# Hidden first pair reloaded for its sums, first product split by chunks, raw weight chunks loaded into the sums' tiles, side copies pinned

## The chip, the cores and the metric

The kernel runs on one NeuronCore of one Trainium2 chip. The metric is the device time of one launch in microseconds. TensorE (PE in the profile) multiplies, VectorE (DVE), ScalarE (ACT) and GpSimd (POOL) work beside it, and SyncE (SP) issues nearly all DMA transfers, in the order of its queue.

## The reference, cut to what matters

One layer of a decoder trunk on 1024 prompt tokens and 64 sample tokens, width 1024: a half-step SwiGLU feed-forward, a token mixer of two branches, a second half-step feed-forward, and a final norm. All in fp32.

```python
def swiglu(x, w_in, w_out):               # D_MODEL 1024, D_FF 2816
    gu = x @ w_in
    g, u = gu[..., :D_FF], gu[..., D_FF:]
    return (jax.nn.silu(g) * u) @ w_out
...
        x = x + 0.5 * swiglu(rmsnorm(x, norm_ffn1[l]), ffn1_w_in[l], ffn1_w_out[l])
...
            rmsnorm(x, norm_mix[l]), pool_hist, out_pos0, conv_hist, h0, w_in[l], pool_w_group[l],
...
    y_prompt = rmsnorm(xp, norm_final)
    y_sample = rmsnorm(xs, norm_final)
```

## The kernel before, in words

**Numbers.** Every fp32 operand is split into a rounded part (`hi`, `hh`, `wh`: ACT copies it to the type fp32r) and a rest (`lo`, `hr`, `wl`: DVE subtracts). A product is three matmuls: high by high, low by high, high by low. Weights arrive by DMA as "raw" chunks (`wraw`, a ring of N_RAW = 6), become `wh` on ACT and `wl` on DVE (rings of N_W = 3 each), and are used once.

**Stages.** By the trace: operands and some plain products of the first feed-forward up to about 105 us; the rest of its first matrix product (`ffn_in`) to 544; `second`, its second matrix product, to 788; the mixer to 2174; the second feed-forward's `ffn_in` to about 2655, its `second` to about 2885; the final norm to the end. Both feed-forwards run the same code. The tokens are worked in two halves h of 512 and 576, each again cut in two so that seven products of a Strassen-Winograd scheme take the place of eight.

**The hidden rows.** For each block ff of 128 hidden columns `hidden` gets the tile g (`L691`). Even blocks go to DRAM at once (a "put" into `hblock`), odd blocks too, and `hidden_odd` then starts a chain `sums` (`L707`): four subtractions in place on the even and odd tiles, each issued H_PACE after the last, then two more puts. A chain is a generator with a due time on a clock that counts PE's issued matmul columns (`pe[0]`); `tick` runs the chain that is due first. The four subtractions run on POOL, except for the first pair (ff == 1), where they run on DVE (`L713`). The last pair is held back (`hlast`) and worked at the start of `second`.

**The second product.** `second` runs the products in the order 1, 2, 5, 6, 4, 7, 3. Each has four units m, each unit 11 steps of k in three chunks of 4, 4 and 3. In a step six matmuls are issued, three for each half. By the trace a unit takes 8.25 us, a chunk of four steps 3.0 us. `fetch_X` (`L731`) issues the loads of a product's operands from `hblock`, tiles `hr` and `hp`, and `split_X` (`L747`) splits them: `hh` on ACT (`L750`), the rest in place on DVE (`L751`). `weights` (`L773`) makes the weights: product 5 adds two raw chunks on POOL (`L785`) into a tile ws that is held, product 6 subtracts another raw chunk from it in place (`L789`), `fourth` (`L800`) turns the held tile into the weights of product 3 in place, and product 7 subtracts two raw chunks into a tile of a ring `wsum` of N_S = 4 (`L794`). `old` (`L812`) adds an earlier part of the result, reloaded as `xo`. `parts` (`L767`, `L768`) then makes `wh` and `wl`.

**Side work.** `part` (`L307`) loads chunks of the mixer's weights during `ffn_in`, waits PART_W, splits them (`ph` by ACT through `split`, `L357`; the rest by DVE, `L359`) and puts both parts in DRAM for the mixer.

**The order.** A scheduler orders each engine's instructions by dependences and priorities; `tc.keep_in_program_order` holds an instruction at its place in the program, `tc.high_priority` moves one ahead. On a queue an instruction that waits holds up all behind it: SP's loads too. `norm_parts` makes the mixer's operands of one half (`L1022`), beginning with the PE sums `pss` of the squares `ssq` (`L386`).

## Time and profile before

| | |
|---|---|
| three runs | 2931.96, 2939.40, 2940.15 us; median 2939.40, mean 2937.17 |
| the profiled execution | 2934.26 us, its span 2932.5 us |
| PE busy | 2793.1 us, 95% of the span |
| DVE, ACT, POOL busy | 1876.5, 1399.6, 1349.2 us |
| mean granted PE clock | 0.982 |
| DMA | 512.47 MB, 175 GB/s over the span |

The span is the profiled execution from its first to its last instruction; what lies around it is 1.8 us. In rows of the timeline a start and a duration come first, then engine, source line, operation and tiles; in brackets stands the idle time of that engine ahead of the row, and what ended it. In rows of windows stand the window, its length, the busy time of PE, of PE's weight loads, DVE, ACT and POOL (with counts), the granted clock, the mean busy share of the DMA engines, and GB/s.

### The profile page before, as it was taken

The page shows a single profiled execution, that of the slowest core. Times are in us where ns is not written, and L with a number is a line of the kernel's source. Part 1 is how long each engine was busy: PE and PEld are TensorE (multiplying, and loading weights), DVE is VectorE, ACT ScalarE, POOL GpSimd, SP SyncE. Part 2 cuts the span into 40 slices and gives each one's busy share as a digit, 9 for nine tenths or more (in the row PEclk, how much of TensorE's full clock was granted, in tenths as well). Part 3 has the DMA queues.
Part 4 walks back from the last instruction along what each step waited for, and adds up shares of the span by engine and source line. Part 5 has one row for each costly group of instructions (what it writes and reads, how often), then busy time and mean ns, then how long its engine had stood idle before and what let it go on. Part 6 is the DMA issues. An engine that isn't in the chain of part 4 may idle for free. (4 is left out here: it accounts for less than half of the span.)

```text
span 2932.5 us, 54478 instructions
## 1 busy us (share of the span) xinstructions
PE 2793.1 (95%) x19834; PEld 2614.3 (89%) x19834; DVE 1876.5 (64%) x2864; ACT 1399.6 (48%) x3086; POOL 1349.2 (46%) x1408
## 2 busy tenths in 40 slices
PE   7999999899999999999989999898999999999998
PEld 6988899899889999999988887677998999998987
DVE  6665554676884486866766767866665554555865
ACT  5444444443454555554546567566233444444434
POOL 5455566345542364554622332323234665561651
PEclk9999999999999999999999999999999999999999
DMA  4576542687545455543366667786774332335873
GB/s 124 163 237 199 183 133 93 185 239 224 184 114 166 158 173 179 183 136 127 103 239 195 191 227 234 252 256 188 232 240 144 101 108 89 100 122 179 243 240 109
DMA packets 564749, 512.47 MB, mean 175 GB/s; under 512 B 37748, under 2 KB 433384, under 8 KB 564472
## 3 DMA queue, kind: packets, MB, share of 16 engines
q1 hardware_dynamic: 564464, 508.98, 55.4%
q8 instruction: 156, 2.56, 0.4%
q14 instruction: 113, 0.93, 0.1%
q10 hardware_dynamic: 16, 0.00, 0.0%
HBM read 361.28 MB, written 147.80 MB: 174 GB/s over the span
## 5 line engine op out<-in xcount | busy, mean ns | idle before, releaser
L166 PE MATMUL pw<-X,wh 128*128 128x288 f32 (+2 forms) x2832 | 625.9, 310 | 3.8 <-ACT v L566 3.5
L166 PEld LDWEIGHTS pw<-X,wh 128*128 128x128 f32 x2832 | 461.5, 189 | 25.6 <-ACT v L566 4.2
L166 PE MATMUL pw<-X,wl 128*128 128x288 f32 (+1 forms) x1644 | 473.2, 288 | 0.9 <-DVE wl L450 0.9
L166 PE MATMUL pw<-hl,wh 128*128 128x256 f32 (+1 forms) x1536 | 393.9, 329 | 6.2 <-DVE t L570 6.2
L450 DVE TENSOR_TENSOR wl<-s,wh 128x512 fp32r<-128x512 f32 x288 | 234.0, 813 | 257.1 <-ACT wh L449 233.3
L443 POOL TENSOR_TENSOR s<-wraw,wraw 128x512 f32<-128x512 f32 x144 | 194.2, 1349 | 336.0 <-DVE wl L450 204.8
L166 PE MATMUL pw<-hi,wl 128*128 128x288 f32 x1120 | 330.8, 295 | 5.1 <-DVE wl L450 5.1
L166 PE MATMUL pw<-hi,wh 128*128 128x288 f32 x1120 | 332.1, 297 | 2.8 <-DVE t L604 2.8
L166 PE MATMUL pw<-lo,wh 128*128 128x288 f32 x1120 | 330.5, 295 | 0.0
L166 PEld LDWEIGHTS pw<-X,wl 128*128 128x128 f32 x1644 | 311.2, 189 | 1.1 <-DVE wl L450 1.1
L166 PE MATMUL pw<-hl,wl 128*128 128x256 f32 x1072 | 301.2, 281 | 0.0
L166 PEld LDWEIGHTS pw<-hl,wh 128*128 128x128 f32 x1536 | 259.8, 190 | 28.1 <-DVE t L570 7.3
L450 DVE TENSOR_TENSOR wl<-wraw,wh 128x512 fp32r<-128x512 f32 x216 | 189.4, 877 | 139.7 <-ACT wh L449 131.5
L449 ACT ACTIVATE wh<-s 128x512 fp32r<-128x512 f32 x288 | 181.1, 630 | 163.6 <-PE pw L166 138.9
L166 PEld LDWEIGHTS pw<-hi,wh 128*128 128x128 f32 x1120 | 211.5, 189 | 9.8 <-DVE t L604 3.5
L166 PEld LDWEIGHTS pw<-hi,wl 128*128 128x128 f32 x1120 | 211.0, 188 | 5.3 <-DVE wl L450 5.3
L166 PEld LDWEIGHTS pw<-lo,wh 128*128 128x128 f32 x1120 | 211.6, 189 | 0.0
L449 ACT ACTIVATE wh<-wraw 128x512 fp32r<-128x512 f32 x216 | 135.5, 628 | 157.6 <-PE pw L166 140.2
L166 PEld LDWEIGHTS pw<-hl,wl 128*128 128x128 f32 x1072 | 203.9, 190 | 0.0
L166 PE MATMUL po<-hh,wl 128*128 128x256 f32 (+1 forms) x848 | 186.8, 292 | 8.6 <-DVE wl L768 8.6
L166 PE MATMUL po<-hh,wh 128*128 128x256 f32 (+1 forms) x848 | 187.1, 291 | 3.8 <-ACT wh L767 3.8
L166 PE MATMUL po<-hr,wh 128*128 128x256 f32 (+1 forms) x848 | 186.2, 290 | 0.0
(399 smaller groups left out, 6839.0 us busy)
## 6 DMA issues: line engine op xcount, KB each, us to landing
wraw<-in_ffn_w_in_dram SPq DMA_DIRECT2D x188, 256.0 KB
wraw<-in_ffn_w_out_dram SPq DMA_DIRECT2D x144, 256.0 KB
wraw<-in_w_in_dram SPq DMA_DIRECT2D x144, 256.0 KB
wh<-part SPq DMA_DIRECT2D x116, 256.0 KB
wl<-part SPq DMA_DIRECT2D x116, 256.0 KB
hr<-hb SPq DMA_DIRECT2D x106, 272.0 KB
hb<-g SPq DMA_DIRECT2D x66, 288.0 KB
hb<-g SPq DMA_DIRECT2D x66, 256.0 KB
```

Of the source, the lines that this page charges most:

```text
L166: T.matmul(out, lhsT, rhs, start=start, stop=stop, skip_group_check=free)
L443: G.tensor_tensor(t, a, b, op=op)
L449: S.activation(wh, a, AF.Copy)
L450: V.tensor_tensor(wl, a, wh.bitcast(F32), op=ALU.subtract)
```

## The change

Six edits, all in both feed-forwards:

1. Of the first pair of hidden blocks both halves of g are put in DRAM at once ("18" and "23" instead of "1" and "23"). A chain `again` starts 100 units of the PE clock later for half 0 and 115 later for half 1: it loads both tiles again (two DMAs for each half), waits H_LOAD = 5, and then runs the sums on POOL, as for all other pairs. DVE has no hidden sums left.
2. H_AT, the delay of the sums' chains, goes from 3 to 4.
3. In `part` the ACT copy is an `AF.Copy` with its place pinned; before it was an `AF.Identity` that the scheduler placed. Counted in the built order, the ACT copy of the chunk for which ACT waits at 345.56 us stood 18 matmuls behind its load's issue before, and stands 61 behind it now. Most others move from 17 to 25 matmuls to 36 to 65; a few stay at 17.
4. In product 1, unit 0, the operands are split by chunks: k 0 to 3 ahead of the unit, k 4 to 7 ahead of its second chunk, the rest ahead of its third.
5. Product 5 loads its first raw chunk into the tile ws and adds the second one in place. Product 7 and `fourth` load one of theirs into a `wsum` tile. So a sum takes one slot of the raw ring and not two, and `fourth` none.
6. `norm_parts` of half 1 for the mixer starts 3.0 later.

```diff
@@ -43,7 +43,7 @@
-H_AT, H_PACE, H_OUT = 3.0, 0.5, 3.0
+H_AT, H_PACE, H_OUT, H_AGAIN, H_LOAD = 4.0, 0.5, 3.0, 100.0, 5.0
 AHEAD = {'2': 11, '5': 11, '6': 8, '4': 8, '7': 10, '3': 10}
...
 STEP_S = 1.0
@@ -303,6 +303,7 @@
         return wh.rearrange("p (k c) -> p k c", c=ncol), wl.rearrange("p (k c) -> p k c", c=ncol)
...
     parted, nth = {}, [0]
+    pin = tc.keep_in_program_order
...
@@ -312,7 +313,8 @@
                 w[k0 * P : (k0 + nk) * P, c0 : c0 + P].rearrange("(k p) c -> p k c", p=P))
...
             a = fx(F32R, "ph")[:, : nk * P]
-            split(t, a, t.bitcast(F32R))
+            pin(S.activation(a, t, AF.Copy))
+            V.tensor_tensor(t.bitcast(F32R), t, a.bitcast(F32), op=ALU.subtract)
             to = [dp.tile([P, nk * P], F32, tag=nm("part"), name=nm("part")) for _ in range(2)]
...
             dma(to[1], t)
@@ -677,8 +679,8 @@
-    for ps_ in ("1", "23", "75", "46"):
-        for i in range(NK2):
+    for i in range(NK2):
+        for ps_ in ("1" if i else "18", "23", "75", "46"):
             t = dp.tile([P, len(ps_), N2], F32, tag=f"hb{ps_}_{i}", name=f"hb{ps_}_{i}")
...
             for j, p in enumerate(ps_):
@@ -687,36 +689,48 @@
+        n, at = NPAIR[h], HALF_AT[h]
         if ff == NFF - 1:
             hlast.append(lambda: hidden_odd(h, ff, g))
+        elif ff == 1:
+            put(h, 0, "23", g)
+            hsums.append(start(again(h), H_AGAIN + 15.0 * h))
         elif ff % 2:
             hidden_odd(h, ff, g)
+        elif ff:
+            even[h] = g
+            dma(hblock["1", ff // 2][:, at : at + n], g[:, :n])
         else:
-            even[h] = g
-            n, at = NPAIR[h], HALF_AT[h]
-            dma(hblock["1", ff // 2][:, at : at + n], g[:, :n])
+            put(h, 0, "18", g)
+
+    def put(h, i, ps_, x):
+        n, at = NPAIR[h], HALF_AT[h]
+        return dma(hblock[ps_, i][:, :, at : at + n], x[:, : 2 * n].rearrange("p (a t) -> p a t", a=2))
+
+    def again(h):
+        n, at = NPAIR[h], HALF_AT[h]
+        e, g = fx(name="e"), fx(name="g")
+        for t, ps_ in ((e, "18"), (g, "23")):
+            dma(t[:, : 2 * n].rearrange("p (a t) -> p a t", a=2), hblock[ps_, 0][:, :, at : at + n])
+        yield H_LOAD
+        yield from pair_sums(h, 0, e, g)
...
-        n, i, at = NPAIR[h], ff // 2, HALF_AT[h]
+        put(h, ff // 2, "23", g)
+        hsums.append(start(pair_sums(h, ff // 2, even[h], g), H_AT))
+
+    def pair_sums(h, i, e, g):
+
+        n = NPAIR[h]
         f, s_ = slice(0, n), slice(n, 2 * n)
-
-        def put(ps_, x):
-            return dma(hblock[ps_, i][:, :, at : at + n], x[:, : 2 * n].rearrange("p (a t) -> p a t", a=2))
-
-        e = even[h]
-        put("23", g)
-
-        def sums():
-            for out, a, b in ((e[:, s_], e[:, s_], e[:, f]), (g[:, s_], g[:, s_], e[:, s_]),
-                              (e[:, f], g[:, s_], e[:, f]), (g[:, f], g[:, f], g[:, s_])):
-                tc.keep_in_program_order((V if ff == 1 else G).tensor_tensor(out, a, b, op=ALU.subtract))
-                yield H_PACE
-            yield H_OUT
-            for ps_, x in (("75", e), ("46", g)):
-                tc.keep_in_program_order(put(ps_, x))
-
-        hsums.append(start(sums(), H_AT))
+        for out, a, b in ((e[:, s_], e[:, s_], e[:, f]), (g[:, s_], g[:, s_], e[:, s_]),
+                          (e[:, f], g[:, s_], e[:, f]), (g[:, f], g[:, f], g[:, s_])):
+            pin(G.tensor_tensor(out, a, b, op=ALU.subtract))
+            yield H_PACE
+        yield H_OUT
+        for ps_, x in (("75", e), ("46", g)):
+            pin(put(h, i, ps_, x))
...
@@ -747,11 +761,12 @@
         def split_X(below=NK2):
...
                 _, r, a = raws.pop(0)
-                tc.keep_in_program_order(S.activation(a, r, AF.Copy))
+                pin(S.activation(a, r, AF.Copy))
                 V.tensor_tensor(r.bitcast(F32R), r, a.bitcast(F32), op=ALU.subtract)
-        def raw(par, mh, m, kb, nk):
-            t = sp.tile([P, 4 * P], F32, tag="wraw", bufs=N_RAW, name=nm("wraw"))[:, : nk * P]
+        def raw(par, mh, m, kb, nk, t=None):
+            if t is None:
+                t = sp.tile([P, 4 * P], F32, tag="wraw", bufs=N_RAW, name=nm("wraw"))[:, : nk * P]
             c0 = (mh * 4 + m) * P
...
             return t
@@ -780,7 +795,7 @@
                     a = raw(*{"1": (0, 0), "2": (1, 0), "4": (1, 1)}[p], m, kb, nk)
...
                     a = held[m, kb] = act((P, 4 * P), name="ws")[:, : nk * P]
-                    x, y = raw(0, 1, m, kb, nk), raw(1, 1, m, kb, nk)
+                    x, y = raw(0, 1, m, kb, nk, a), raw(1, 1, m, kb, nk)
                     with tc.high_priority(hp[0]):
...
                 elif p == "6":
@@ -789,14 +804,15 @@
                         G.tensor_tensor(a, a, x, op=ALU.subtract)
...
                     a = stage["p"].tile([P, 4 * P], F32, tag="wsum", bufs=N_S, name=nm("ws"))[:, : nk * P]
-                    x, y = raw(0, 0, m, kb, nk), raw(0, 1, m, kb, nk)
+                    x, y = raw(0, 0, m, kb, nk, a), raw(0, 1, m, kb, nk)
                     with tc.high_priority(hp[0]):
...
             for kb, nk in chunks:
-                a, x = held[m, kb], raw(1, 0, m, kb, nk)
+                t = stage["p"].tile([P, 4 * P], F32, tag="wsum", bufs=N_S, name=nm("ws"))[:, : nk * P]
+                a, x = held[m, kb], raw(1, 0, m, kb, nk, t)
                 G.tensor_tensor(a, x, a, op=ALU.subtract)
...
         def old(m, q, col):
@@ -816,7 +832,9 @@
         def unit(p, m, hs, ws):
...
             for kb, nk, wh, wl in ws:
-                if kb == 8 and len(hs) == 2:
+                if kb and len(hs) == 2 and (p, m) == ("1", 0):
+                    split_X(kb + 4)
+                elif kb == 8 and len(hs) == 2:
                     split_X()
...
                     k = kb + kk
@@ -864,13 +882,14 @@
                 add(a[:, s_], a[:, s_])
...
         fetch_X("1", NK2)
-        split_X()
+        split_X(4)
         while hlast:
...
         for p, nxt in zip(order[:-1], order[1:]):
-            split_X(8)
+            if p != "1":
+                split_X(8)
             fetch_X(p, NK2)
...
                 if p == "6":
@@ -1025,7 +1044,7 @@
         o = []
...
         finish(c)
-        prep1m[h] = start(norm_parts(xt, h, i_gm, o, (0.5, 1.2)[h], s), 0.0), o
+        prep1m[h] = start(norm_parts(xt, h, i_gm, o, (0.5, 1.2)[h], s), (0.0, 3.0)[h]), o
...
```

How the built order moves, at three places. New line numbers are higher: `L783` is the old `L768`, `L765` the old `L751`, `L771` the old `L756`, `L757` the old `L743`, `L800` the old `L785`, `L804` the old `L789`. Behind an arrow stand the operands.

VectorE at the start of product 1 in the first feed-forward, before: `hr` are the operands' rests, `wl` of 128x512 and 128x384 the weights of the second and third chunk of unit 0.

```order
L751 TENSOR_TENSOR hr_6300<-hr_6300,hh_6299 128x544
L751 TENSOR_TENSOR hr_6303<-hr_6303,hh_6302 128x544
L609 TENSOR_TENSOR g_6176<-g_6176,pw_1090_6162 128x288
L751 TENSOR_TENSOR hr_6306<-hr_6306,hh_6305 128x544
L751 TENSOR_TENSOR hr_6309<-hr_6309,hh_6308 128x544
L751 TENSOR_TENSOR hr_6312<-hr_6312,hh_6311 128x544
L751 TENSOR_TENSOR hr_6315<-hr_6315,hh_6314 128x544
L751 TENSOR_TENSOR hr_6318<-hr_6318,hh_6317 128x544
L751 TENSOR_TENSOR hr_6321<-hr_6321,hh_6320 128x544
L751 TENSOR_TENSOR hr_6324<-hr_6324,hh_6323 128x544
L768 TENSOR_TENSOR wl_6397<-wraw_6394,wh_6396 128x512
L768 TENSOR_TENSOR wl_6427<-wraw_6424,wh_6426 128x384
```

The same place in the changed kernel:

```order
L783 TENSOR_TENSOR wl_6361<-wraw_6358,wh_6360 128x512
L608 TENSOR_TENSOR g_6184<-pw_1106_6230,t_6183 128x288
L765 TENSOR_TENSOR hr_6308<-hr_6308,hh_6307 128x544
L765 TENSOR_TENSOR hr_6311<-hr_6311,hh_6310 128x544
L611 TENSOR_TENSOR g_6184<-g_6184,pw_1094_6170 128x288
L783 TENSOR_TENSOR wl_6391<-wraw_6388,wh_6390 128x512
L783 TENSOR_TENSOR wl_6429<-wraw_6426,wh_6428 128x384
L765 TENSOR_TENSOR hr_6314<-hr_6314,hh_6313 128x544
L765 TENSOR_TENSOR hr_6317<-hr_6317,hh_6316 128x544
L765 TENSOR_TENSOR hr_6320<-hr_6320,hh_6319 128x544
L765 TENSOR_TENSOR hr_6323<-hr_6323,hh_6322 128x544
L783 TENSOR_TENSOR wl_6470<-wraw_6467,wh_6469 128x512
```

The `wl` of chunks 2 and 3 stood behind all eleven `hr`; now they stand behind the fourth, and the `hr` of k 4 to 7 behind them.

SyncE's queue ahead of product 7 in the first feed-forward, before: 8518 to 8524 are the raw chunks of the last `fourth`, 8542 and 8544 the two of product 7's first sum, 8576 to 8612 those of its second and third.

```order
L756 DMA wraw_8518<-in_ffn_w_out_dram 128x4x128
L756 DMA wraw_8521<-in_ffn_w_out_dram 128x4x128
L756 DMA wraw_8524<-in_ffn_w_out_dram 128x3x128
L756 DMA wraw_8542<-in_ffn_w_out_dram 128x4x128
L743 DMA hr_8414<-hb_6_294 128x544
L743 DMA hr_8417<-hb_7_295 128x544
L743 DMA hr_8420<-hb_8_296 128x544
L756 DMA wraw_8544<-in_ffn_w_out_dram 128x4x128
L756 DMA wraw_8576<-in_ffn_w_out_dram 128x4x128
L756 DMA wraw_8578<-in_ffn_w_out_dram 128x4x128
L756 DMA wraw_8610<-in_ffn_w_out_dram 128x3x128
L756 DMA wraw_8612<-in_ffn_w_out_dram 128x3x128
```

The same stretch in the changed kernel: 8420 to 8480 are the last weights of product 4, 8539 to 8605 the second raw chunks of product 7's first three sums, 8658 to 8724 those of its unit 1.

```order
L771 DMA wraw_8420<-in_ffn_w_out_dram 128x4x128
L771 DMA wraw_8450<-in_ffn_w_out_dram 128x4x128
L771 DMA wraw_8480<-in_ffn_w_out_dram 128x3x128
L771 DMA wraw_8539<-in_ffn_w_out_dram 128x4x128
L771 DMA wraw_8572<-in_ffn_w_out_dram 128x4x128
L771 DMA wraw_8605<-in_ffn_w_out_dram 128x3x128
L771 DMA wraw_8658<-in_ffn_w_out_dram 128x4x128
L757 DMA hr_8410<-hb_6_292 128x544
L757 DMA hr_8413<-hb_7_296 128x544
L757 DMA hr_8416<-hb_8_300 128x544
L771 DMA wraw_8691<-in_ffn_w_out_dram 128x4x128
L771 DMA wraw_8724<-in_ffn_w_out_dram 128x3x128
```

The first raw chunks of unit 0's three sums (into `wsum` tiles) and the last `fourth`'s three stand 20 and more rows further ahead now; three loads of `hr` stand behind the four second chunks instead of ahead of them.

POOL in products 5 and 6 of the first feed-forward, before: 7520 to 7588 are the sums of product 5's unit 3, `L789` the subtractions of product 6.

```order
L785 TENSOR_TENSOR ws_7440<-wraw_7441,wraw_7443 128x512
L785 TENSOR_TENSOR ws_7474<-wraw_7475,wraw_7477 128x384
L785 TENSOR_TENSOR ws_7520<-wraw_7521,wraw_7523 128x512
L785 TENSOR_TENSOR ws_7554<-wraw_7555,wraw_7557 128x512
L785 TENSOR_TENSOR ws_7588<-wraw_7589,wraw_7591 128x384
L789 TENSOR_TENSOR ws_7178<-ws_7178,wraw_7638 128x512
L789 TENSOR_TENSOR ws_7212<-ws_7212,wraw_7669 128x512
L789 TENSOR_TENSOR ws_7246<-ws_7246,wraw_7700 128x384
L789 TENSOR_TENSOR ws_7290<-ws_7290,wraw_7750 128x512
```

And in the changed kernel, where 7519 to 7585 are the same three sums of unit 3:

```order
L804 TENSOR_TENSOR ws_7328<-ws_7328,wraw_7777 128x512
L804 TENSOR_TENSOR ws_7361<-ws_7361,wraw_7808 128x384
L804 TENSOR_TENSOR ws_7408<-ws_7408,wraw_7860 128x512
L804 TENSOR_TENSOR ws_7441<-ws_7441,wraw_7891 128x512
L800 TENSOR_TENSOR ws_7519<-ws_7519,wraw_7521 128x512
L800 TENSOR_TENSOR ws_7552<-ws_7552,wraw_7554 128x512
L800 TENSOR_TENSOR ws_7585<-ws_7585,wraw_7587 128x384
L804 TENSOR_TENSOR ws_7474<-ws_7474,wraw_7922 128x384
L804 TENSOR_TENSOR ws_7519<-ws_7519,wraw_7972 128x512
```

The three sums of product 5's unit 3 stood ahead of all of product 6; now they stand behind the eight subtractions for its units 0, 1 and most of 2. The order is the same in the second feed-forward. One more move on SyncE, ahead of product 5: the six raw chunks of its unit 0 stood ahead of the `hp` load that waits for PE's last unit of product 2, all but the second chunk of the third sum, which came three loads behind it (an `hp` and two `hr`). Now the second chunks of all three sums stand ahead of that load, and the first chunks of all three behind it and the two `hr`.

## The prediction

> **What bounds the kernel now.** PE is busy for 95% of the span, so a gain can come only from PE's idle stretches and from the clock that falls behind them. I read the windows of the profile stage by stage, then PE's list of waits, then the timeline around each wait. The windows in which this change can act, and four others that matter below:
>
> ```profile
> 60.00:105.00 45.00, 39.70 (x243) 36.27 (x243) 35.20 (x53) 20.60 (x47) 23.34 (x21) 0.96 0.40 113
> 343.00:352.00 9.00, 4.43 (x19) 4.07 (x20) 4.33 (x7) 2.68 (x6) 2.53 (x4) 0.81 0.90 293
> 541.00:586.00 45.00, 37.16 (x275) 36.48 (x275) 27.84 (x37) 20.91 (x41) 10.07 (x9) 0.92 0.57 174
> 718.00:755.00 37.00, 28.74 (x195) 27.42 (x194) 23.85 (x31) 13.61 (x24) 25.39 (x22) 0.91 0.96 279
> 800.00:820.00 20.00, 16.05 (x66) 11.84 (x65) 15.71 (x26) 9.05 (x21) 13.33 (x12) 0.91 0.20 55
> 2240.00:2255.00 15.00, 9.93 (x61) 9.52 (x60) 8.43 (x12) 4.17 (x8) 6.66 (x5) 0.89 0.49 148
> 2655.00:2700.00 45.00, 39.09 (x284) 38.32 (x284) 26.28 (x34) 20.23 (x41) 10.02 (x9) 0.89 0.53 164
> 2828.00:2862.00 34.00, 27.95 (x178) 26.36 (x177) 19.68 (x28) 12.48 (x21) 21.23 (x19) 0.85 0.94 279
> 615.00:630.00 15.00, 15.00 (x122) 15.00 (x121) 9.12 (x13) 5.70 (x10) 6.33 (x5) 1.00 0.95 274
> 630.00:645.00 15.00, 15.00 (x122) 15.00 (x121) 11.38 (x16) 5.39 (x10) 8.67 (x7) 1.00 0.94 257
> 690.00:705.00 15.00, 15.00 (x122) 15.00 (x121) 10.87 (x16) 6.24 (x11) 8.87 (x8) 1.00 0.60 181
> 705.00:718.00 13.00, 13.00 (x106) 13.00 (x105) 4.27 (x7) 2.84 (x5) 5.04 (x4) 1.00 0.67 197
> ```
>
> Each of the first eight loses twice: length less PE's busy time is idle, and length times (1 less the clock) is at most what the lower clock cost. For 718 to 755 that is 8.26 idle and 3.3 clock, for 2828 to 2862 6.05 and 5.1, for 2240 to 2255 5.07 and 1.7, for 343 to 352 4.57 and 1.7. The clock part is an upper bound, since a slow clock costs nothing while PE waits. The list of waits names the second products as the largest payer:
>
> ```profile
> PE po L166 <- ACT wh L767: 16.2, 10, 3.3
> ...
> PE po L166 <- DVE wl L768: 10.5, 6, 4.9
> ```
>
> **Start of the first feed-forward.** DVE does three hidden sums ahead of a weight that PE wants:
>
> ```profile
> 77.78 1.97 DVE L713 TENSOR_TENSOR g<-g,g 128x256 f32<-128x256 f32 x2
> 79.68 1.01 DVE L713 TENSOR_TENSOR g<-g 128x256 f32<-128x256 f32 x1
> 80.61 0.68 DVE L297 TENSOR_TENSOR wl<-wraw,wh 128x512 fp32r<-128x512 f32 x1
> ...
> 81.35 0.63 PE L166 MATMUL pu<-hi,wl 128*128 128x288 f32 x2 [2.54 <-DVE wl L297]
> ```
>
> Without them (1.97 + 1.01 = 2.98 us) the weight is there in time: 2.54 and up to 1.8 of clock. In the new order one other DVE operation moves ahead of an earlier weight, about 0.6 back. I take -3.0, bounds -4.3 and +1. The eight sums of each feed-forward go to POOL about 130 us later, where others of their kind cost about 1.2 us (below); DVE and POOL are both far from full, and nothing wants the sums before product 5 or later, 400 us on. The reload adds four loads and a larger put for each feed-forward, some 272 KB each, at a place where the transfers are not the bound. I take +1 in all, bounds 0 and +3.
>
> The GPSIMD Engine Reference of the Trainium skill (Specifications) says that GpSimd shares its SBUF interfaces with VectorE, and contends with vector instructions that have two SBUF inputs. The rows of 545.58 below agree (1.20 us beside POOL, 0.68 without). By it the sixteen moved sums would slow what DVE does beside them, by at most 16 x 1.2 x (1 - 0.68 / 1.20) = 8 us of DVE time, estimated, which the idle share of DVE covers.
>
> **The wait on a put in the second feed-forward** goes with the same edit. DVE's in-place sum waits for the put of the tile that it overwrites, and a weight stands behind it:
>
> ```profile
> 2245.85 1.40 DVE L713 TENSOR_TENSOR g<-g,g 128x288 f32<-128x288 f32 x1 [5.69 <-DMA hb<-g]
> ...
> 2248.97 0.53 PE L166 MATMUL pw<-hi,wl 128*128 128x288 f32 x1 [5.07 <-DVE wl L450]
> ```
>
> DVE does no hidden sums now: -5.07 and -1.7 of clock, so -6.7, bounds -6.8 and -4 (if another operation brings part of it back).
>
> **Side copies.** One copy holds ACT, and through it the evictions that PE waits for:
>
> ```profile
> 345.56 0.63 ACT L357 ACTIVATE ph<-pr 128x512 fp32r<-128x512 f32 x1 [7.66 <-DMA pr<-in_w_o_dram]
> ...
> 347.57 0.56 PE L166 MATMUL pw<-hl,wh 128*128 128x512 f32 x1 [4.59 <-DVE t L570]
> ```
>
> This copy now stands 61 matmuls behind its load instead of 18, at 0.16 us each (39.70 us over 243 in the first window) 10 us against 3. ACT waited 7.66, so 7 more is nearly all of it, and the rest falls in ACT's own slack. I take -4.6 - 1.7 = -6.3, bounds -6.3 and 0.
>
> **The mixer's start.** Half 1's `pss` waits for its squares:
>
> ```profile
> 810.40 1.23 PE L166 MATMUL pss<-ones,ssq 128*128 128x1 f32 x10 [2.65 <-DVE ssq L386]
> ```
>
> With 3.0 more delay it stands behind other matmuls, and the chain of half 1 ends some 3 us later, which costs nothing as long as half 0's operands feed PE. I take -2.65 and 1.8 of clock: -4.4, bounds -4.4 and -1.4 (the 3 us paid in full).
>
> TensorE: Matmul & The Clock Gate of the Trainium skill (HAM oscillation — how this bites in real kernels) sets the limit for PE's idle gaps at about 3.4 us. The rows differ: this gap is 2.65, and the clock in its window is 0.91. By that rule the clock parts at 81, here and in product 7 would have another cause than the gaps; that is a rival below.
>
> **First product.** DVE makes all eleven operands' rests ahead of the second chunk's weight, and POOL's sums of the last hidden pair slow it:
>
> ```profile
> 542.49 0.40 PE L166 MATMUL pw<-hi,wh 128*128 128x288 f32 x1 [1.48 <-DVE t L604]
> ...
> 544.19 0.41 PE L166 MATMUL po<-hh,wh 128*128 128x256 f32 x2
> ...
> 555.27 0.82 PE L166 MATMUL po<-hh,wl 128*128 128x256 f32 x2 [4.86 <-DVE wl L768]
> ...
> 543.95 1.35 DVE L751 TENSOR_TENSOR hr<-hr,hh 128x544 fp32r<-128x544 f32 x2
> 545.22 0.45 DVE L609 TENSOR_TENSOR g<-g,pw 128x288 f32<-128x288 f32 x1
> 545.58 8.43 DVE L751 TENSOR_TENSOR hr<-hr,hh 128x544 fp32r<-128x544 f32 x7
> 553.94 2.94 DVE L768 TENSOR_TENSOR wl<-wraw,wh 128x512 fp32r<-128x512 f32 x3
> ...
> 554.63 1.24 POOL L713 TENSOR_TENSOR g<-g 128x288 f32<-128x288 f32 x1
> ```
>
> In the new order, from 545.6: two `wl` at 0.98, done at 547.6, when PE ends its first chunk (544.19 + 3.0). Then four `hr` at 1.20, a `wl`, three `hr`, one or two of them at 0.68 behind POOL's end: about 556.5, plus one step of 0.75 is 557.2. Unwaited the unit would end at 544.2 + 8.25 = 552.4, so 4.75 of its loss stays. Before, it lost 7.84 - 1.48 (a wait ahead of it, unchanged) = 6.4 and some 2.7 of the 3.6 of clock: -4.3. In the second feed-forward 5.91 + 3.4 of 4.95 - 4.75: -4.6. Together -8.9, bounds -4 and -13.
>
> **Product 7.** Its sums wait for raw chunks that stand late in SP's queue, as the ring of six is held by two for each sum:
>
> ```profile
> 714.30 7.64 SPq L756 DMA_DIRECT2D wraw<-in_ffn_w_out_dram  x6
> ...
> 719.42 2.83 POOL L794 TENSOR_TENSOR ws<-wraw,wraw 128x512 f32<-128x512 f32 x2 [3.46 <-DMA wraw<-in_ffn_w_out_dram]
> ...
> 721.05 0.63 ACT L767 ACTIVATE wh<-ws 128x512 fp32r<-128x512 f32 x1 [1.91 <-POOL ws L794]
> ...
> 721.73 0.78 PE L166 MATMUL po<-hp,wh 128*128 128x256 f32 x4 [3.30 <-ACT wh L767]
> ```
>
> In the new queue the chunks of the first three sums are issued some 10 us earlier, and chunks for four sums (the `wsum` ring) fit ahead instead of for three. All of it would be 11.6 and 11.1. But the transfers are near their limit: 705 to 755 took 0.67 x 13 + 0.96 x 37 = 44.2 us of full-rate time. Without the stalls there are 50 - 11.6 = 38.4 us, at 0.95 36.5, and 690 to 705 has room for 0.35 x 15 = 5.3: short by 2.4. I leave 3 us in each: -8.6 and -8.1, so -16.7, bounds -6 and -22.7.
>
> **What product 5 pays.** The first chunks of its unit 0 now stand behind the held-up `hp` load, where one second chunk stood before:
>
> ```profile
> 613.35 2.06 SPq L756 DMA_DIRECT2D wraw<-in_ffn_w_out_dram  x1
> ...
> 618.81 1.01 POOL L785 TENSOR_TENSOR ws<-wraw,wraw 128x384 f32<-128x384 f32 x1 [6.25 <-PE po L166]
> ...
> 619.27 0.66 PE L166 MATMUL po<-hp,wh 128*128 128x256 f32 x4
> ```
>
> From that issue to the sum's start were 5.5 us. So the first sum starts at 618.8 now, takes 1.3, `wh` 0.63: ready at 620.8, `wl` at 621.5, where PE wants them at 619.3. I take +1.75 in each feed-forward, bounds 0 and 4. Behind it, unit 3's sums stand behind eight of product 6's subtractions on POOL, and in a full stretch (0.95 and 0.94 of the transfers, 257 GB/s):
>
> ```profile
> 636.66 1.30 POOL L785 TENSOR_TENSOR ws<-wraw,wraw 128x512 f32<-128x512 f32 x1 [0.35 <-DVE x L837]
> ...
> 643.39 13.47 POOL L789 TENSOR_TENSOR ws<-ws,wraw 128x512 f32<-128x512 f32 x9 [1.76 <-DMA wraw<-in_ffn_w_out_dram]
> ```
>
> The eight need 1.97 MB more ahead of unit 3's chunks: 7.6 us at 257 GB/s. So its first sum starts at 636.66 + 7.6 = 644.3, its `wl` is there at 646.9, and PE wants it at 619.3 + 3 x 8.25 + 1.75 = 645.8: +1 in each. If the eight run in a row behind unit 2 they take 8 x 1.50 = 12 us, and it is +6.6. One fallen clock stretch for each feed-forward adds 1.7. Together 2 x (1.75 + 1 + 1.7) = +8.9, bounds 0 and +24.
>
> **Sum.** -3.0 - 6.7 - 6.3 - 4.4 - 8.9 - 16.7 = -46.0; +8.9 + 1.0. Net -36.1 from the profiled 2934.3: 2898. The three runs' mean is 2.9 above that execution and their median 5.1, so I forecast 2900 for a median.
>
> **Rivals.**
>
> *Transfers are the bound in products 5 to 7.* For it: 0.94 to 0.96 in four of the windows above; the bytes are the same and the time for them shrinks. Against it: 690 to 718 and 586 to 615 have room. Product 7 then gives 6 and product 5 costs 14: 2934 - 46 + 10.7 + 14 + 1 = 2914, some 2916 as a median. 0.24.
>
> *All gains, no new wait.* 2934 - 3.6 - 6.7 - 6.3 - 4.4 - 10 - 22.7 = about 2880. For it: POOL is idle in 31% to 58% of the windows 615 to 645 and 718 to 755. Against it: the row of 618.81. 0.12.
>
> *The side copies and the start do not change* (pinned copies wait elsewhere, and hold ACT there): 9.3 and 4.4 less, 2912. For it: a few copies still stand 17 matmuls behind their loads. 0.08.
>
> *The clock stays low where only short gaps go.* The 1.8 at 81, 1.8 at 810 and 3.3 and 5.1 in product 7 are then not won: 2900 + 10 to 12 = 2911. Against it: each of those windows has both the gap and the lower clock, and the four windows without a gap have 1.00. 0.04.
>
> *Slower: product 5 and 6 work in lock step.* Place: POOL's eight subtractions ahead of unit 3. Each waits for a raw chunk, whose slot comes free only with the subtraction before, whose load then takes 5.5 us as above: 8 x (5.5 + 1.5) = 56 us where PE brings 25 of work. That is up to 31 late in each feed-forward: 2900 + 2 x 31 - 4 = 2958. It decides from 18 us late in each. Against it: six slots, not one. 0.07.
>
> **How the numbers follow.** The forecast has 0.41 (2888 to 2908), the rivals 0.24, 0.12, 0.08, 0.04 and 0.07; 0.04 is left for gains that cancel near 2935. A measurement of this kernel can tell about 0.3%, 9 us, from no change: faster is under 2930.6. Faster gets the first five but for a twentieth, 0.84; the same 0.08; slower 0.08, the last rival and the edge of what cancels. The range runs from the second rival's 2880 to 2926, which takes in the first, third and fourth with 10 us above them.
>
> **What would show it.** In the changed profile: no DVE row of hidden sums, and none of 5.07 on PE near 2244; no 7.66 of ACT on `pr`; a `wl` of the second chunk right behind the fourth `hr`, and unit 0 of product 1 paced by DVE; product 7 without waits of 3 us on `wh`; new waits of 1 to 2 us on `wh` at the start of product 5 and at its unit 3. I am wrong if product 5's waits pass 8 us in each feed-forward, or product 7's stay.

## The result, and the profile after

Twelve runs of each kernel: 2933.5 us (2925.5 to 2941.6) with the change, 2937.7 us (2923.6 to 2941.1) before. The ratio of the means is 0.9994, with a 95% interval of 0.9979 to 1.0009: no difference clear of the scatter. The forecast was 2900. The profiled execution of the changed kernel has a span of 2927.9 us, 4.6 below the one of before, and PE is busy for 95% of it, as it was.

The list of PE's waits in the changed kernel, longest in sum first (sum, times, longest). Before, the line of `po` and `wh` read 16.2, and the one of `po` and `wl` 10.5:

```profile
PE po L166 <- ACT wh L782: 24.2, 7, 7.2
PE ptx L166 <- DVE dg L962: 11.6, 1, 11.6
PE pst L166 <- DVE xd L1564: 9.2, 4, 5.2
PE pgm L166 <- DMA d<-dh: 7.4, 1, 7.4
PE po L166 <- DVE hr L765: 6.7, 13, 1.4
PE ptr L170 <- DMA xin<-in_x_prompt_dram: 6.3, 3, 4.3
```

The waits for `wl` have left the top, as forecast. But the waits for `wh` grew, with a single one of 7.2 us, and the transposes' wait for `xin` has one of 4.3. To see where, I cut both traces at the first matmul of each stage and unit and took the lengths (us):

| stretch | before | after | change |
|---|---|---|---|
| start to `ffn_in` | 108.6 | 102.3 | -6.3 |
| `ffn_in`, about the first half of its matmuls | 210.6 | 220.6 | +10.0 |
| `ffn_in`, the rest, to product 1 | 225.0 | 218.2 | -6.8 |
| product 1, unit 0 | 17.3 | 13.6 | -3.7 |
| product 2's last unit and product 5 | 41.3 | 52.8 | +11.5 |
| product 4's last unit, product 7 | 54.2 | 45.9 | -8.3 |
| product 3 to the end of `second` | 35.3 | 41.3 | +6.1 |
| mixer, to the second `ffn_in`'s first winograd matmul | 1436.1 | 1436.9 | +0.8 |
| second `ffn_in` | 419.8 | 412.6 | -7.2 |
| second feed-forward, unit 0 of product 1 | 17.9 | 13.4 | -4.5 |
| its product 2's last unit and product 5 | 41.2 | 52.3 | +11.1 |
| its product 4's last unit, product 7 | 53.6 | 46.2 | -7.4 |

("Winograd matmul" is one of the products `pw` of the Strassen-Winograd scheme.) What is left out differs by 0.5 or less. The gains add up to 44.2, against 46.0 forecast. The losses add up to 39.5, against 9.9.

**The losses, read in the trace.** Unit 3 of product 5. PE's row, POOL's rows ahead of it, then SyncE's:

```profile
646.81 0.58 PE L166 MATMUL po<-hp,wh 128*128 128x256 f32 x1 [7.18 <-ACT wh L782]
...
630.79 8.80 POOL L804 TENSOR_TENSOR ws<-ws,wraw 128x512 f32<-128x512 f32 x6 [3.20 <-DMA wraw<-in_ffn_w_out_dram]
640.06 1.26 POOL L804 TENSOR_TENSOR ws<-ws,wraw 128x512 f32<-128x512 f32 x1 [0.47 <-DMA wraw<-in_ffn_w_out_dram]
642.41 1.26 POOL L804 TENSOR_TENSOR ws<-ws,wraw 128x512 f32<-128x512 f32 x1 [1.09 <-DMA wraw<-in_ffn_w_out_dram]
644.83 1.26 POOL L800 TENSOR_TENSOR ws<-ws,wraw 128x512 f32<-128x512 f32 x1 [1.16 <-DMA ws<-in_ffn_w_out_dram]
...
619.97 19.04 SPq L771 DMA_DIRECT2D wraw<-in_ffn_w_out_dram  x12
639.06 0.97 SPq L757 DMA_DIRECT2D hr<-hb  x2
640.08 0.43 SPq L771 DMA_DIRECT2D ws<-in_ffn_w_out_dram  x1
```

The eight subtractions of product 6 (`L804`) run ahead of unit 3's first sum (`L800`), as the built order said. The first chunk of that sum is issued only at 640.08, behind twelve raw loads that took SyncE 19 us. From 618 to 641 SyncE's loads waited 10.9 us in all for slots that POOL's subtractions (`L804`, 6.1) and sums (`L800`, 4.8) free. The windows of the same stretch:

```profile
615.00:630.00 15.00, 14.89 (x119) 14.89 (x120) 12.51 (x17) 6.49 (x12) 9.40 (x7) 1.00 1.16 300
630.00:645.00 15.00, 9.63 (x77) 9.40 (x76) 6.51 (x7) 2.17 (x4) 11.49 (x9) 0.96 0.59 171
```

From 630 to 645 the transfers are down to 0.59, where they were at 0.94 before. So the queue stands still, and not because the transfers are full. (A share above 1 means that transfers are counted whole in the window in which they start.)

Near 211, SyncE's rows, then PE's:

```profile
190.03 0.53 SPq L992 DMA_DIRECT2D xin<-in_x_sample_dram  x1
200.58 0.38 SPq L471 DMA_DIRECT2D wraw<-in_ffn_w_in_dram  x1
...
205.03 2.81 SPq L708 DMA_DIRECT2D hb<-g  x4
207.94 3.51 SPq L1001 DMA_DIRECT2D xspill<-xr  x4
211.50 0.71 SPq L992 DMA_DIRECT2D xin<-in_x_prompt_dram  x1
...
215.61 0.90 PE L170 MATMUL ptr<-ident,xin 128*128 128x128 f32 x3 [4.32 <-DMA xin<-in_x_prompt_dram]
```

From 190.6 to 200.6 SyncE waits for one weight load's slot, 9.9 us of it for a weight sum on POOL, and puts and loads leave in a bunch behind it. From 190 to 201 the share of the transfers is 0.07, where it was 0.69 before. Two waits on evictions (copies out of a finished product) follow. The one of 2.29 us at 227.79 stands on ACT behind a row that waited 3.33 us for POOL, and POOL had just worked three weight sums whose loads left from 214.66 on, in that bunch. The one of 3.52 us at 261.34 comes after a second hold of SyncE, 6.6 us up to 254.7, again for a weight sum. Behind it a side copy stalled in a new place:

```profile
259.33 0.63 ACT L316 ACTIVATE ph<-pr 128x512 fp32r<-128x512 f32 x1 [6.59 <-DMA pr<-in_w_o_dram]
...
261.34 0.66 PE L166 MATMUL pw<-hl,wh 128*128 128x512 f32 x1 [3.52 <-DVE t L572]
```

Product 3 of the first feed-forward:

```profile
755.64 0.43 SPq L293 DMA_DIRECT2D wraw<-in_w_in_dram  x1
760.59 0.32 SPq L1038 DMA_DIRECT2D xspill<-x  x1
760.95 0.92 SPq L757 DMA_DIRECT2D hr<-hb  x2
...
763.99 0.66 ACT L764 ACTIVATE hh<-hr 128x544 fp32r<-128x544 f32 x1 [6.33 <-DMA hr<-hb]
...
766.83 0.58 PE L166 MATMUL po<-hh,wh 128*128 128x256 f32 x1 [4.64 <-ACT wh L782]
```

Two operand loads stand behind a put of the result that is not ready until 760.59. In the built order of before they stood ahead of it. The second feed-forward makes no such put, and has no such wait.

### The profile page after: what moved, and what is told of

Same layout as the page of the kernel before. It is cut to its first block, busy times and chain, and to the rows that moved or that the text cites. A ratio compares the mean times of both kernels' runs of the same rounds, so it can differ in the third digit from the quotient of the medians.

```text
span 2927.9 us, 54569 instructions
## 1 busy us (share of the span) xinstructions
PE 2787.8 (95%) x19834; PEld 2608.0 (89%) x19834; DVE 1851.4 (63%) x2848; ACT 1400.3 (48%) x3086; POOL 1367.9 (47%) x1424
## 5 line engine op out<-in xcount | busy, mean ns | idle before, releaser
L445 POOL TENSOR_TENSOR s<-wraw,wraw 128x512 f32<-128x512 f32 x144 | 201.2, 1397 | 340.5 <-DVE wl L452 218.2
L452 DVE TENSOR_TENSOR wl<-wraw,wh 128x512 fp32r<-128x512 f32 x216 | 174.0, 806 | 138.6 <-ACT wh L451 130.6
L166 PEld LDWEIGHTS pw<-hi,wl 128*128 128x128 f32 x1120 | 210.6, 188 | 0.0
L166 PE MATMUL pso<-yhl,wh 128*128 128x288 f32 (+1 forms) x768 | 180.8, 338 | 5.7 <-ACT acc L1795 3.6
```

Of the source, the lines that this page charges most:

```text
L166: T.matmul(out, lhsT, rhs, start=start, stop=stop, skip_group_check=free)
L445: G.tensor_tensor(t, a, b, op=op)
L452: V.tensor_tensor(wl, a, wh.bitcast(F32), op=ALU.subtract)
```

## The experiments

But for the delay of edit 6 the mixer is the same in all of these kernels, and took 1435.6 to 1444.7 us from `second`'s end to the second `ffn_in`'s first winograd matmul. So single spans compare within some 9 us; waits and stage lengths say more.

**1. Product 5's order on POOL.** Both POOL operations pinned:

```diff
-                        G.tensor_tensor(a, x, y, op=ALU.add)
+                        pin(G.tensor_tensor(a, x, y, op=ALU.add))
...
-                        G.tensor_tensor(a, a, x, op=ALU.subtract)
+                        pin(G.tensor_tensor(a, a, x, op=ALU.subtract))
```

> The changed kernel with the sums of product 5 and the subtractions of product 6 held in the order of the program on POOL, so that unit 3's three sums stand ahead of all of product 6 again. Loads, tiles and bytes stay. Theory A (POOL's order is what makes product 5 late): the PE waits of 7.2 us near 640 and 5.0 us near 2751 fall under 1 us, the two waits of 1.3 to 1.4 us at unit 0 stay, the span falls by 14 to 17 us (7.2 + 5.0 and two stretches of half clock). Theory B (the transfers are the bound there, the order only follows them): a wait of 4 us or more stays at one of the units 1 to 3 of product 5, or comes back in product 6, and the span falls by less than 6 us.

Neither. Units 1 to 3 of product 5 have no wait of a microsecond any more, so POOL's order made unit 3 late, as theory A has it. But the span is 2944.7, longer by 17. A wait of 5.99 us stands now at the start of product 4, and one of 7.15 in the second feed-forward:

```profile
692.86 1.28 PE L166 MATMUL po<-hp,wh 128*128 128x256 f32 x4 [5.99 <-ACT wh L782]
```

**2. Product 5 through the ring**, as it was before:

```diff
-                    x, y = raw(0, 1, m, kb, nk, a), raw(1, 1, m, kb, nk)
+                    x, y = raw(0, 1, m, kb, nk), raw(1, 1, m, kb, nk)
```

> The changed kernel with product 5 as before: both raw chunks through the ring, none straight into the sum's tile. Theory A (this edit alone costs product 5): the waits at unit 0 (1.3 and 1.4 us) and at unit 3 (7.2 and 5.0 us) are all gone, product 5 takes 33.0 us in both feed-forwards as before, and the span falls by 17 to 22 us. Theory B (the earlier loads of products 6 and 7 crowd product 5, whatever its tiles): waits of 3 us or more stay in products 5 or 6, and the span falls by less than 8 us.

Product 5 takes 33.0 us in both feed-forwards again, with no wait at all: the first half of theory A. The span is 2931.4, and the waits are at product 4, 5.28 and 3.18 us. Here its cause can be read:

```profile
670.67 9.15 SPq L771 DMA_DIRECT2D ws<-in_ffn_w_out_dram  x8
679.87 0.95 SPq L874 DMA_DIRECT2D x<-xspill  x2
680.86 0.91 SPq L757 DMA_DIRECT2D hr<-hb  x2
...
685.33 1.45 ACT L764 ACTIVATE hh<-hr 128x544 fp32r<-128x544 f32 x2 [11.14 <-DMA hr<-hb]
...
687.35 1.04 PE L166 MATMUL po<-hp,wh 128*128 128x256 f32 x3 [5.28 <-ACT wh L782]
```

Eight of `fourth`'s loads, which take sum tiles from a ring of four, are queued ahead of product 4's operands, and wait for POOL to use the tiles up. ACT waits 11.14 us for those operands. In the changed kernel `fourth`'s loads hold SyncE there too (7.21 us from 670.06, 7.86 from 680.27), and product 4 starts without a wait; that product 5 is late enough to cover it is my reading. The transfers of the stretch are at 0.43 (660 to 675), so the second theory's crowding is not the cause.

**3. Product 3's loads first.** They and the result's puts are pinned:

```diff
-                dma(r, hblock[p, k])
+                d = dma(r, hblock[p, k])
+                if p == "3":
+                    pin(d)
...
-                dma(xspill[h][4 + i], x[:, :N])
+                pin(dma(xspill[h][4 + i], x[:, :N]))
```

> The changed kernel with the operand loads of product 3 held ahead of the puts of the first feed-forward's result on SyncE. Theory A (two operand loads stand behind a put that waits for its result, which cost the 4.6 us wait at 762): that wait goes, unit 1 of product 3 in the first feed-forward starts 5 to 6.5 us earlier against unit 0, and the span falls by 4 to 6.5. Theory B (those loads are late because the transfers are full): the wait stays at 3 us or more.

Theory A: the wait is gone, nothing over 0.2 us is left between 755 and 775, unit 1 of product 3 starts 8.7 us after unit 0 against 14.5, and the span is 2923.3, 4.6 lower.

**4. The reloaded pair's sums on VectorE**, at the same place:

```diff
-        yield from pair_sums(h, 0, e, g)
+        yield from pair_sums(h, 0, e, g, V)
...
-    def pair_sums(h, i, e, g):
+    def pair_sums(h, i, e, g, eng=G):
...
-            pin(G.tensor_tensor(out, a, b, op=ALU.subtract))
+            pin(eng.tensor_tensor(out, a, b, op=ALU.subtract))
```

> The changed kernel with the reloaded pair's sums on VectorE in place of POOL, at the same place; its loads and puts stay. Theory A (eight more sums fill POOL near 190 to 200 and 245 to 255, raw slots come free late, and SyncE's queue with them): the waits of SyncE of 9.9 and 6.6 us for POOL's sums of weights shrink to 6 and less, the PE waits of 4.3 us at 211, 2.3 at 225 and 3.5 at 258 fall to 5 us in all or less, and the stretch from 190 to 285 is 5 to 10 us shorter. Theory B (the traffic of reload, larger put and their places in SyncE's queue cost it): the three waits stay at 8 us or more in all.

Between the two. SyncE's waits for POOL's weight sums from 184 to 262 fall from 17.3 to 13.8 us. The three PE waits are 2.25, 2.41 and 2.87, 7.5 in all, and the stretch from 142 to 319 is 3.6 us shorter. POOL's extra sums are a part of it and not the most.

**5. `fourth` through the ring as well**, on top of the second experiment:

```diff
-                t = stage["p"].tile([P, 4 * P], F32, tag="wsum", bufs=N_S, name=nm("ws"))[:, : nk * P]
-                a, x = held[m, kb], raw(1, 0, m, kb, nk, t)
+                a, x = held[m, kb], raw(1, 0, m, kb, nk)
```

> The second experiment's kernel with the raw chunk of `fourth` through the raw ring as well, so that only product 7 loads into the four sum tiles. Theory A (with product 5 mended the loss came back at product 4, because the loads of `fourth` wait for sum tiles and stand ahead of product 4's operands on SyncE): the waits of 5.3 us at 682 and 3.2 us at 2796 go, products 2 to 4 take 33.0 us each, product 7 keeps most of its gain (waits under 4 us in all), and the span is 12 to 18 us below the changed kernel's 2927.9. Theory B (the transfers of products 5 to 7 need that time wherever it is taken): 5 us or more of waits come back in product 4 or 7, and the span is within 6 us of 2927.9.

Products 2 to 4 run without a wait, as theory A says, yet the span is 2927.0: theory B's number. The waits come back in product 7, 6.3 us and 7.4 us. This is the longest of the first feed-forward, with the windows around it:

```profile
727.37 0.52 PE L166 MATMUL po<-hh,wh 128*128 128x256 f32 x2 [2.88 <-ACT wh L782]
...
690.00:705.00 15.00, 15.00 (x122) 15.00 (x121) 8.54 (x14) 5.22 (x9) 5.53 (x5) 1.00 0.48 135
705.00:720.00 15.00, 13.28 (x102) 12.62 (x101) 7.62 (x10) 5.22 (x9) 8.20 (x6) 1.00 0.92 283
720.00:735.00 15.00, 11.71 (x76) 10.95 (x75) 6.78 (x11) 3.08 (x6) 10.39 (x11) 0.89 1.01 303
```

Ahead of product 7 ten raw loads hold SyncE from 687.68 for 16.92 us, with the transfers at 0.48; in it they come in a burst, 0.92 to 1.01. Against the second kernel, product 7 with the unit ahead of it takes 53.2 us and not 46.9 (52.3 and not 46.5 in the second feed-forward). So product 7 had its gain from `fourth`'s use of the sum tiles, which leaves the raw slots free, and that same use holds the queue up ahead of product 4.

**6. The reload 100 units later:**

```diff
-H_AT, H_PACE, H_OUT, H_AGAIN, H_LOAD = 4.0, 0.5, 3.0, 100.0, 5.0
+H_AT, H_PACE, H_OUT, H_AGAIN, H_LOAD = 4.0, 0.5, 3.0, 200.0, 5.0
```

> The changed kernel with the pair's reload 100 units later (H_AGAIN 200), so that its loads, sums and puts fall behind the transposes' loads and xspill puts of 160 to 255. Theory A (where the reload falls costs it: POOL's sums and its transfers together): the PE waits at 211, 225 and 258 (10.1 us in the changed kernel) fall to 4 us or less, the stretch from the 10th to the 50th part of `ffn_in`'s matmuls (142 to 323) shortens by 6 to 11 us, and nothing of that size comes back later. Theory B (the pinned side copies cost it, as two of the three waits follow an ACT copy of `pr`): the waits at 225 and 258 stay at 4 us or more together.

The waits at 225 and 258 are gone; one of 1.67 us, for the transposes, is left at 231.49. The stretch is 6.3 us shorter. So these two are the reload's. The wait near 211 stays, 4.58 us, and is not. The span is 2933.5 all the same: the mixer took 7.5 us longer than in the changed kernel, and the second product 5 has a longer wait, 7.08 us against 5.03.

**7. The side copies as before**, on the changed kernel:

```diff
-            pin(S.activation(a, t, AF.Copy))
-            V.tensor_tensor(t.bitcast(F32R), t, a.bitcast(F32), op=ALU.subtract)
+            split(t, a, t.bitcast(F32R))
```

> The changed kernel with the side copies as before (Identity, placed by the scheduler). Theory A (pinning them won the 4.6 us wait near 343 and its half clock, and does not cause the waits at 211 to 258): a wait of 4 us or more on an eviction comes back near 343, the waits at 211 to 258 stay within 3 us of 10.1 in all, and the span is 3 to 8 us longer. Theory B (the pinned copies moved the wait from 343 to 225 and 258): these two waits go, 343 comes back, and the span stays within 2 us.

Theory A, and more than it asked: the wait near 343 is back (4.54 us at 360.44), the three earlier ones come to 11.6, and the span is 2948.9, 21 longer. Of this 16.7 stands ahead of product 1, 14.4 of it in `ffn_in`.

**8. Three causes mended at once:** the diffs of experiments 2, 5, 6 and 3 in one kernel.

> The fifth experiment's kernel with the later reload and with product 3's loads held ahead of the puts. If the causes found are separate, the waits of each are gone at once and the span comes to 2927.9 less 15 (products 5 and 4), less 8 (reload) and less 5 (product 3), about 2900, between 2894 and 2908. If a wait only moves to the next place each time, it is above 2915.

2913.3, between the two statements: 14.6 of the hoped 28 us. What is left is product 7 (7.0 us of waits in the first feed-forward) and the wait near 208, 4.72 us.

**9. The kernel before with the pins alone:**

```diff
-            split(t, a, t.bitcast(F32R))
+            tc.keep_in_program_order(S.activation(a, t, AF.Copy))
+            V.tensor_tensor(t.bitcast(F32R), t, a.bitcast(F32), op=ALU.subtract)
```

> The kernel before with edit 3 alone (side copies pinned, AF.Copy). Theory A (the pins win the wait near 343, and pay part of it back, because in the order that they give a weight load that waits for POOL's sums stands ahead of the puts and of the transposes' loads on SyncE): the 4.6 us wait near 343 goes, the wait of 1.5 us for the transposes' load near 212 grows to 3.5 to 5, SyncE waits 7 us or more for a sum of POOL between 185 and 205, and the span is 0 to 5 us below 2932.5. Theory B (the wait near 212 is the reload's): it stays at 1 to 2 us, and the span is 5 to 8 us lower.

Theory A in its waits: near 343 nothing is left, SyncE waits 9.7 us for a POOL sum between 184 and 214, and the transposes' wait grows from 1.48 to 7.27, more than the 3.5 to 5 expected:

```profile
SPq L470 <- POOL s L444: 9.7, 1, 9.7
...
219.55 0.69 PE L170 MATMUL ptr<-ident,xin 128*128 128x128 f32 x2 [7.27 <-DMA xin<-in_x_prompt_dram]
```

In the built order, the pins move one weight load ahead of the `xspill` puts and the transposes' loads. Product 1 begins 3.4 us earlier than before, but 2.2 of this stands ahead of `ffn_in`, where nothing was changed; `ffn_in` itself is 1.2 shorter. The span is 2934.8, 2 longer and within the mixer's scatter. Since the seventh kernel, without pins, has the same load ahead, another edit can move it as well.

**10. The kernel before with the tiles alone** (edit 5):

```diff
-        def raw(par, mh, m, kb, nk):
-            t = sp.tile([P, 4 * P], F32, tag="wraw", bufs=N_RAW, name=nm("wraw"))[:, : nk * P]
+        def raw(par, mh, m, kb, nk, t=None):
+            if t is None:
+                t = sp.tile([P, 4 * P], F32, tag="wraw", bufs=N_RAW, name=nm("wraw"))[:, : nk * P]
...
-                    x, y = raw(0, 1, m, kb, nk), raw(1, 1, m, kb, nk)
+                    x, y = raw(0, 1, m, kb, nk, a), raw(1, 1, m, kb, nk)
...
-                    x, y = raw(0, 0, m, kb, nk), raw(0, 1, m, kb, nk)
+                    x, y = raw(0, 0, m, kb, nk, a), raw(0, 1, m, kb, nk)
...
-                a, x = held[m, kb], raw(1, 0, m, kb, nk)
+                t = stage["p"].tile([P, 4 * P], F32, tag="wsum", bufs=N_S, name=nm("ws"))[:, : nk * P]
+                a, x = held[m, kb], raw(1, 0, m, kb, nk, t)
```

> The kernel before with edit 5 alone (raw chunks straight into the sums' tiles of products 5, 7 and `fourth`). Theory A (this edit takes from product 5 and gives to product 7, and gains nothing in sum): product 5 takes 41 to 46 us in place of 33.0 in both feed-forwards, product 7 loses 7 to 9 us less than before, and the span is 2 to 14 us above 2932.5. Theory B (product 5's loss comes from the other edits' earlier start): product 5 takes under 36 us, and the span is 10 us or more below 2932.5.

Theory A: product 5 takes 43.6 and 42.0 us, product 7 with the unit ahead 8.5 and 6.8 less than before, the span is 2944.3, 11.8 longer. So it is this edit, and not the other edits' earlier start:

```profile
651.51 0.82 PE L166 MATMUL po<-hp,wh 128*128 128x256 f32 x2 [6.84 <-ACT wh L768]
```

Product 3's loss is here too, 41.3 us against 35.3, with a wait of 3.68 us at 771.35 behind the same order of put and loads: this edit alone is enough for it.

**11 and 12. Versions timed** against the kernel before, on one chip. The eleventh is the eighth without product 7's tile too, so without any of edit 5:

```diff
-                    x, y = raw(0, 0, m, kb, nk, a), raw(0, 1, m, kb, nk)
+                    x, y = raw(0, 0, m, kb, nk), raw(0, 1, m, kb, nk)
```

> The eighth experiment's kernel without any of edit 5: the later reload, product 3's loads ahead of the puts, the pinned copies, the split by chunks and the later `norm_parts`. Theory A (edit 5 as a whole is worth nothing, and the other edits carry the gain): within 6 us of the eighth experiment's 2913 span, and 0.4 to 0.9% under the kernel before. Theory B (product 7's tiles are still worth their 12 us): 8 us or more slower than it.

> The eighth experiment's kernel again, timed. By the one look it is 17 us, 0.6%, under the kernel before: 0.991 to 0.997 of its time.

The eleventh: 2916.4 us, 0.9941 of the kernel before (0.9921 to 0.9962), and within 3 us of the eighth's span: theory A. The twelfth, the eighth kernel again: 2912.0 us, 0.9932 (0.9912 to 0.9951). Both beat the kernel before, whose runs there had a median of 2932.8. The medians differ by 4.3 us and the intervals overlap, so what product 7's tile is worth by itself is not settled.

## Why the prediction was wrong

**The gains came, but for one term.** Start of the first feed-forward: 3.0 forecast, 6.3 found. The ninth and tenth kernels, which do not touch that stretch, take 106.4 and 106.7 us for it, so some 2 us of the 6.3 is scatter. Side copies: 6.3 against 6.8 in the second half of `ffn_in`, and 7.0 with the pins alone (ninth). Product 7: 16.7 against 15.7. The wait on the put: 6.7 against 7.2 in the second `ffn_in`. First products: 8.9 against 8.2, paced by DVE as described, in rows that follow the walk closely:

```profile
542.72 1.76 DVE L783 TENSOR_TENSOR wl<-wraw,wh 128x512 fp32r<-128x512 f32 x2
544.40 4.78 DVE L765 TENSOR_TENSOR hr<-hr,hh 128x544 fp32r<-128x544 f32 x4
549.10 1.29 DVE L783 TENSOR_TENSOR wl<-wraw,wh 128x512 fp32r<-128x512 f32 x1
550.31 3.78 DVE L765 TENSOR_TENSOR hr<-hr,hh 128x544 fp32r<-128x544 f32 x3
```

That each `hr` takes 1.20 us comes with POOL's rows beside it. In the tenth kernel, whose product 1 is not split, POOL has a single long row there, and seven `hr` take 0.65 us each:

```profile
544.39 4.53 DVE L751 TENSOR_TENSOR hr<-hr,hh 128x544 fp32r<-128x544 f32 x7
...
544.49 6.78 POOL L610 TENSOR_TENSOR g<-g,t 128x288 f32<-128x288 f32 x1 [12.11 <-ACT g L607]
```

(Durations on POOL are rough.) Its unit 0 takes 10.9 us without the split, but later units give this back: from product 1's start to product 2's last unit it takes 66.2 us, against 66.8 before and 63.1 in the changed kernel.

The mixer's start is the term that did not come: 4.4 forecast. The wait at the `pss` went from 2.65 to 1.13 us, but two waits for `wl`, 1.75 us at 838.57 and 1.22 at 842.81, stand where one of 1.46 stood before. The mixer as a whole took 0.8 longer. Its first 300 matmuls took 65.7 us before and 63.8 after, but 65.4 to 67.1 in nine of the ten other kernels that have edit 6, so no gain can be told from the scatter.

**The step that failed is the cost of product 5.** The forecast put +1.75 on unit 0 and +1 on unit 3, with an upper end of 6.6 for the eight subtractions in a row (its own steps give 5.5: 12 us in place of 7.6 adds 4.4 to the 1). With the lowered clock, +8.9 was forecast for both feed-forwards and +22.6 measured. Unit 0 was right (1.34 and 1.37 us waited). Unit 3 waited 7.18 and 5.03. The error was to price the eight by bytes at 257 GB/s, as if transfers went on at the rate of before. They did not: SyncE stood at loads that waited for POOL, and the transfers fell to 0.59. The high end of the bound came from a row of POOL (13.47 us for nine), and was the one to take, because loads ahead of unit 3's wait for slots that these subtractions free. This is the mechanism of the rival that ended slower, on a smaller scale: 11.5 and 11.1 us late, short of the 18 from which it was to decide.

**Two costs were not in the sum.** The reload and the pins together took 10.0 us between 102 and 323, where the forecast had +1. The wait near 211 comes with a weight load that moved ahead in SyncE's queue (shown for the pins alone by the ninth kernel, where this half of `ffn_in` is 5.8 longer), the waits at 225 and 258 with the reload's place (sixth, 6.2 shorter). The forecast costed the pins by ACT alone, and did not follow the queue that they reorder. And product 3's two operand loads moved behind a put, 6.1 us, which the order showed and the forecast did not look at (third and tenth). So edit 5, forecast to win 7.8 in sum (16.7 less 8.9), cost 13.0 (22.6 and 6.1 less 15.7), and by itself made the span 11.8 longer (tenth).

**The rival on transfers** named the right place for a wrong reason. It gave 14 to product 5, and 22.6 was paid there, at a transfer share of 0.59; in the second experiment a share of 0.43 stands beside a wait of 5.28 us at product 4. In product 7 full transfers do stand beside waits, 0.92 and 1.01 in the fifth kernel and 0.96 before. But the changed kernel has 1.08 from 690 to 705 and 1.01 from 720 to 735 with PE busy throughout, so that the transfers are the bound even there is not shown.

**The gain behind a mended wait.** Experiments 1, 2 and 5 mend one wait each, and the span does not follow: the loss goes from product 5 to 4 to 7. That the rings of six and four slots and the one queue pass the same lateness on is my reading: no run changes the size of a ring. The forecast worked out product 5's cost and product 7's gain each for itself, with slack taken from the trace of before.

**On the clock:** around the waits of 1.34 us at unit 0 of product 5 and 1.43 in product 1 the granted clock stayed at 1.00 (605 to 623, 545 to 556), but behind the one of 1.37 at 2724.11 it was 0.83 (2725 to 2735). The waits of 2 us and more came with lowered clocks, as the forecast had it: 0.71 from 216 to 224, 0.79 from 226 to 234, from 260 to 268 and from 766 to 774. In the window of the wait of 7.18, the granted clock is 0.81, while the held-up transfers leave at a share of 0.97:

```profile
645.00:660.00 15.00, 13.19 (x91) 13.03 (x92) 12.07 (x14) 6.37 (x12) 14.37 (x11) 0.81 0.97 292
```

The wait near 208 in the best version was not mended. What another place for that weight load would give was not tried.

## What to carry to other kernels

When an edit moves loads, follow every queue that they pass: list what stands behind each load that waits for a ring slot, and who wants it, in the built order of the changed kernel. Price a stalled queue by the rows of what frees its slots, not by bytes at the bandwidth of before (here 7.18 and 5.03 us, where the bytes gave 1). And where stages share a ring, a gain in one stage counts only once the next stage's slack has been worked out with the earlier start.

## What the runs showed that I had not expected

One weight load, moved by a few places in SyncE's queue, came with waits of 4.3 to 7.3 us at the transposes, since it waits some 10 us for POOL with a dozen loads and puts behind it. Taking the pins from the changed kernel made `ffn_in` 14.4 us longer; adding them to the kernel before made it 1.2 us shorter: an edit's worth depended on the order that the others gave.
